# A hybrid decoder layer: own buffer for a sigmoid, 252-column products, an earlier weight load, banded diagonal sums and another PSUM bank

## The chip, the cores and the metric

The kernel runs on one core of a Trainium2 chip. The metric is the device time of one execution in microseconds (us), the median of several. Engines are named as the profile names them: PE is TensorE's matmul and PEld its weight load, DVE is VectorE, ACT is ScalarE, POOL is GpSimd, and SP issues the DMAs.

## The reference

One inference step of a hybrid layer for 1024 prompt tokens and 8 samples of 4 tokens each. 16 learned meta tokens stand ahead of the prompt and are dropped from its output; in all 1072 tokens of width 1024.

```python
# h = h + W_out( sum_b sigmoid(gate_b(x)) * W_b( silu(zgate_b(x)) * mixer_b(x) ) ),  x = RMSNorm(h)
# four branches, each 512 wide, fed from one combined input projection:
#   A: GLA      gated linear attention, 4 heads of dk 64, dv 128
#   B: HGRN2    4 heads of 128
#   C: mLSTM    4 heads of 128
#   D: convolution: GLU -> causal depthwise conv of width 31 -> LayerNorm -> swish -> pointwise
# gla_chunk: S_t = diag(exp g_t) S_{t-1} + k_t^T v_t ;  o_t = q_t S_t
```

It gives the outputs of both groups and the end states of all four branches.

## The kernel before

Numbers are kept near fp32 by splitting each operand into a high part in the rounded type fp32r and the rest as a low part. A product is then three matmuls: high by high, low by high, high by low. Weights are split by ACT (`wh`, L138) and POOL or DVE (`wl`, L139); `E=V` asks for DVE.

The stages follow one another in time. Up to about 100 us, `x` is normalised, transposed (`xt`, L174) and split (`xh` L178, `xl` L179) in three blocks of 384, 384 and 304 tokens; four gate projections (`gate_direct`) and small projections (`small`) run beside it. Then comes the pair stage until about 500 us: 19 calls of `pair`, each of which computes a 256 x 1072 projection with 7 products instead of 8, in the manner of Strassen. A product is 2 halves of 268 tokens, 4 blocks of k, 3 matmuls: 24, and 168 a pair. The products land in PSUM tiles `sa` to `sd`, and the callbacks `c11`, `c12`, `c22` and `c21` take the four quarters of the result. The names `p1`, `u2`, `u3` and `p5` are their sums, made on DVE.

Four of the 19 pairs (`conv_pair`) make the convolution's input `u`; the other 15 (`pair_to`) make gates and send them out by DMA. In `conv_pair`, `c11` puts a sigmoid of the first quarter into `u` (ACT, L349), `c12` multiplies `u` in place (DVE, L352), and `conv_taps` then runs 31 DVE operations over `u` (L388 for 30 of them), with a priority that lets them fill DVE's free time. `u` and the sum `y` have one buffer each, so that a convolution's `u` is free only when the last tap of the one before has read it.

From 500 us the mixers follow: four HGRN2 units, two GLA units (from about 850 us), four mLSTM units, and at last the branch and gate products until the end. In the GLA units `vtok` projects values (`vf`), transposes them by `to_tok` (`tta`, evacuated by ACT as `vt`, L539) and splits a small transposed piece (`v9p`, L557). `linear_unit` makes diagonal sums (`dg`, L760) with `prod` as weights and a matrix of 2 columns, in plain fp32, which is two instructions a matmul. `lv` (L636) and `lvt` (L640) are the small products of the attention levels.

No order is written out by hand. A scheduler simulates the program's timeline when it is built and sets each engine's order, so a change in one place moves rows elsewhere. PSUM tiles come from pools: `acc_tile` from one with 3 buffers, which the projections use too, `mmt` from another with 3.

Of the kernel before, what the change touches and what calls it, by code (L numbers as in the profile page):

```python
# [27 lines left out]
P = 128  # L28
# [37 lines left out]
def trunk(ctx, tc, hx, w_in, w_sm, w_br, w_out, pk, wgk2, mlb, fnorm, s_gla, s_hg, s_c, s_n, s_m, s_cv,  # L66
# [80 lines left out]
    xh = xp.tile([P, KD, NT], F32R, name="xh", tag="xh")  # L147
    xl = xp.tile([P, KD, NT], F32R, name="xl", tag="xl")
    with tc.tile_pool(name="x0", bufs=9, side="right", reuse_waits="tile") as x0:
        hs = []  # L150

        def load_h(i):
            n = min(P, NT - i * P)
            h = x0.tile([P, D], F32, name="h", tag="h")
            DMA.dma_start(h[:n], hx[i * P:i * P + n, :])
            hs.append((h, n))

        for i0 in (0, 3, 6):
            for i in range(i0, i0 + 3):
                load_h(i)  # L160
                h, n = hs[i]
                ss = x0.tile([P, 1], F32, name="ss", tag="ss", bufs=9)
                sq = x0.tile([P, D], F32, name="sq", tag="sq", bufs=1)
                S.activation(sq[:n], h[:n], AF.Square, accum_out=ss[:n])
                V.tensor_scalar(ss[:n], ss[:n], 1.0 / D, EPS, ALU.mult, ALU.add)
                rs = rsqrt(ss[:n])
                V.tensor_scalar(h[:n], h[:n], rs, None, ALU.mult)
            if i0 == 0:
                raw0 = load_raw(w_in, OFF["gate"])
            for k in range(KD):  # L170
                ps = mmt("xt")
                t = 0
                for h, n in hs[i0:i0 + 3]:
                    T.transpose(ps[:, t:t + n], h[:n, k * P:(k + 1) * P], ident[:n, :n])  # L174
                    t += n
                nw = col("norm_w", k)
                hi = xh[:, k, i0 * P:i0 * P + t]
                S.activation(hi, ps[:, :t], AF.Identity, scale=nw)  # L178
                V.scalar_tensor_tensor(xl[:, k, i0 * P:i0 * P + t], ps[:, :t], nw, hi, ALU.mult, ALU.subtract)  # L179
            if i0 == 0:  # L180
                w0 = split_w(raw0, E=V)

    def mm3(ps, wh, wl, ah, al, kd, order=None):
        for i, k in enumerate(order or range(kd)):
# [23 lines left out]
    def stt(tag, name=None):  # L208
        return gtl(tag, [P, HT], STB[tag], name)
# [39 lines left out]
        xs.update(a11=a(0, 0), a12=a(KH, 0), a22=a(KH, HT), s1=a(0, HT), s2=(sh[:, 0], sl[:, 0]),  # L249
                  s3=(sh[:, 1], sl[:, 1]), s4=(sh[:, 2], sl[:, 2]))  # L250

    def pair(c0, c1, c11, c12, c22, c21):


        wp = pools["gph"]
        r0, r1 = load_raw(w_in, c0), load_raw(w_in, c1)
        b11, b21, b12, b22 = r0[:, :KH], r0[:, KH:], r1[:, :KH], r1[:, KH:]
        w1 = split_w(r0)
        ta = wp.tile([P, KD, P], F32, name="ta", tag="tt", bufs=2)
        t1, t2 = ta[:, :KH], ta[:, KH:]  # L260
        V.tensor_tensor(t1, b12, b11, ALU.subtract)
        V.tensor_tensor(t2, b22, t1, ALU.subtract)
        w2 = split_w(ta, E=V, pool="gph")
        tb = wp.tile([P, KD, P], F32, name="tb", tag="tt", bufs=2)
        t3, t4 = tb[:, :KH], tb[:, KH:]
        V.tensor_tensor(t3, b22, b12, ALU.subtract)
        V.tensor_tensor(t4, b21, t2, ALU.subtract)
        w3 = split_w(tb, E=V, pool="gph")
        w4 = split_w(r1[:, KH:], KH)
        ps = lambda tag: [pools["ps"].tile([P, 512], F32, name="s" + tag, tag="a" if tag == "a" else "r",  # L270
                                           bufs=2 if tag == "a" else 5)[:, :HS] for _ in range(2)]

        def prod(w, o, x, s, out, start, stop):
            xa, xb = (t[:, :, s * HS:(s + 1) * HS] for t in xs[x])
            for k in range(KH):
                wh, wl = w[0][:, o + k], w[1][:, o + k]
                T.matmul(out, wh, xa[:, k], start=start and k == 0, stop=False, skip_group_check=True)  # L277
                T.matmul(out, wh, xb[:, k], start=False, stop=False, skip_group_check=True)  # L278
                T.matmul(out, wl, xa[:, k], start=False, stop=stop and k == KH - 1, skip_group_check=True)  # L279

        h = lambda t, s: t[:, s * HS:(s + 1) * HS]
        a, b, c = ps("a"), ps("b"), ps("c")
        p1, u2 = stt("p1"), stt("u2")
        for s in range(2):
            prod(w1, 0, "a11", s, a[s], True, True)
            S.activation(h(p1, s), a[s], AF.Copy)
        for s in range(2):
            prod(w2, KH, "s2", s, b[s], True, True)
            V.tensor_tensor(h(u2, s), h(p1, s), b[s], ALU.add)
        p5, u3 = stt("p5"), stt("u3")  # L290
        for s in range(2):
            prod(w2, 0, "s1", s, c[s], True, True)
            S.activation(h(p5, s), c[s], AF.Copy)
        for s in range(2):
            prod(w1, KH, "a12", s, a[s], False, True)
            c11(s, a[s])
        d = ps("d")
        for s in range(2):
            prod(w3, 0, "s3", s, d[s], True, True)
            S.activation(h(u3, s), d[s], AF.Copy)  # L300
        V.tensor_tensor(u3, u3, p5, ALU.add)
        V.tensor_tensor(u3, u3, u2, ALU.add)
        c22(u3)
        for s in range(2):
            prod(w4, 0, "s4", s, c[s], False, True)
            V.tensor_tensor(h(p1, s), h(u2, s), c[s], ALU.add)
        c12(p1)
        for s in range(2):
            prod(w3, KH, "a22", s, d[s], False, True)
            V.tensor_tensor(h(u2, s), h(u2, s), d[s], ALU.add)  # L310
        c21(u2)

    def pair_to(sec, i, dst, func, times=False, base=0):

        g11 = stt("g11")
        o = OFF[sec] + i * P
        i += base

        def c11(s, ps):
            g = g11[:, s * HS:(s + 1) * HS]  # L320
            S.activation(g, ps, func)
            if times:
                V.tensor_tensor(g, ps, g, ALU.mult)
            if s == 1:
                DMA.dma_start(dst[i, :, 0:HT - NM], g11[:, NM:])

        def rest(j, second):
            def ev(t):
                if times:
                    sg = stt("sg")  # L330
                    S.activation(sg, t, func)
                    V.tensor_tensor(t, t, sg, ALU.mult)
                elif func != AF.Copy:
                    S.activation(t, t, func)
                if second:
                    DMA.dma_start(dst[j, :, HT - NM:], t)
                else:
                    DMA.dma_start(dst[j, :, 0:HT - NM], t[:, NM:])
            return ev

        pair(o, o + P, c11, rest(i + 1, False), rest(i + 1, True), rest(i, True))

    def conv_pair(i):
        u = gtl("u", [P, UW + NSEQ * 34])
        us = u[:, UW:].rearrange("p (s x) -> p s x", x=34)
        G.memset(u[:, 0:30], 0.0)

        def c11(s, ps):
            S.activation(u[:, 30 + s * HS:30 + (s + 1) * HS], ps, AF.Sigmoid)  # L349

        def c12(t):
            V.tensor_tensor(u[:, 30:30 + HT], t, u[:, 30:30 + HT], ALU.mult)  # L352

        held = []

        def c21(t):
            S.activation(t, t, AF.Sigmoid)
            m = NP - HT
            V.tensor_tensor(u[:, 30 + HT:UW], held[0][:, :m], t[:, :m], ALU.mult)
            x3 = lambda v: v[:, m:].rearrange("p (s j) -> p s j", j=NDEC)  # L360
            V.tensor_tensor(us[:, :, 30:34], x3(held[0]), x3(t), ALU.mult)

        pair(OFF["cb"] + i * P, OFF["ca"] + i * P, c11, c12, held.append, c21)
        return u, us
# [73 lines left out]
                DMA.dma_start(fscr[p, :, t0:t0 + n], gx)  # L438

    open_pool("gph", bufs=1)  # L440
    gate_direct(0, w=w0)
    gate_direct(1)
    small()
    for j in range(2, NDIR):
        gate_direct(j)
# [129 lines left out]
    def vtok(sec, i, ones_col=False):  # L575
        vf = tl("vf", [P, 9 * P], 1)
        G.memset(vf[:, NT:NT + 16], 0.0)
        x9 = tl("x9", [P, 3, NT - NP], 1)

        def ev(ps, t0, n):  # L580
            S.activation(vf[:, t0:t0 + n], ps, AF.Copy)
            if t0 + n == NT:
                S.activation(x9, ps[:, NP - t0:].unsqueeze(1).broadcast_to([P, 3, NT - NP]), AF.Copy)

        proj(sec, i, GA, ev)
        vt = tl("vt", [P, 9, 129], 4)
        (to_tok_v(vf, vt) if ones_col else to_tok(vf, vt, True))
        v9 = split3(x9, 1, "v9", 4, acc_tile("v9p"))
        if ones_col:
            G.memset(vt[:, :, 128:129], 1.0)  # L590
        return vt, v9
# [162 lines left out]
    def linear_unit(uid, qv, nh, k, f, prod, vts, s0, epss, finish, pout, sout):  # L754
        rw = P // nh
        if nh == 2:
            ps = mmt("dg")
            for c in range(9):
                n = csz(c)
                T.matmul(ps[:n, 2 * c:2 * c + 2], prod[:, c * P:c * P + n], onesb, start=True, stop=True)  # L760
            dg = tl("dg", [P, 18], 2)
            V.tensor_copy(dg[:, 0:16], ps[:, 0:16])
            V.tensor_copy(dg[:TAIL, 16:18], ps[:TAIL, 16:18])
# [583 lines left out]
```

## Time and profile before

| | |
|---|---|
| median of 3 runs | 1597.33 us (1597.06 to 1597.72) |
| the profiled execution | 1597.18 us |
| its span in the profile | 1595.4 us |
| mean granted TensorE clock | 0.989 |
| PE, DVE, ACT, POOL busy | 98%, 65%, 35%, 30% of the span |

The profile is one execution. A row of a group gives busy us and the mean of one in ns, then the idle time before them and what ended it. A row of a timeline gives the start and duration in us, and in brackets the idle time ahead of it and its releaser. A matmul's duration is from issue to the last result; since matmuls overlap, their rate is read from how many start in a stretch.

### The profile page before, as it was taken

To read this page: it belongs to the slowest core of one execution; us is meant where nothing else is said; L and a number is where in the kernel's file an instruction comes from. 1 tells how busy PE (TensorE), PEld (TensorE's weight loads), DVE (VectorE), ACT (ScalarE), POOL (GpSimd) and SP (SyncE) were. 2 spreads that over 40 slices of the span, in tenths; PEclk is the share of its full clock that TensorE was granted. 3 is DMA by queue.
4 is the path that set the end of the run, shared out by engine and by line. 5 is a ranking of instruction groups with operands and counts; after the bars stand their busy time and mean duration, and the time that the engine had idled before them with its cause. 6 is when DMAs were issued, how large, how long until landed. Compare 5 with 4: busy or idle time off the path is not lost.

```text
span 1595.4 us, 30033 instructions
## 1 busy us (share of the span) xinstructions
PE 1558.2 (98%) x12366; PEld 1496.5 (94%) x12366; DVE 1035.6 (65%) x1827; ACT 554.0 (35%) x1095; POOL 470.9 (30%) x418
## 2 busy tenths in 40 slices
PE   7999999899999999999999999999999999999998
PEld 6999999899999899999998998999999999999886
DVE  7959979999996446444544565476665646744533
ACT  6534343243433333323424323323323244422211
POOL 2222322123223232223232323222322313877300
PEclk9999999999999999999999999999999999999999
DMA  5423233231337113131323132144323277676231
GB/s 190 133 80 101 92 91 107 88 108 51 110 100 236 42 48 104 56 100 56 104 60 94 55 97 82 49 148 135 117 72 88 89 248 224 179 236 208 80 111 54
DMA packets 190572, 176.40 MB, mean 111 GB/s; under 512 B 9260, under 2 KB 164800, under 8 KB 190436
## 3 DMA queue, kind: packets, MB, share of 16 engines
q1 hardware_dynamic: 190436, 174.49, 35.6%
q8 instruction: 97, 1.59, 0.4%
q14 instruction: 39, 0.32, 0.1%
HBM read 122.45 MB, written 52.00 MB: 109 GB/s over the span
## 4 chain that ended last, share of the span: by engine, by line
PE 78%; DVE 16%; issue 3%; DMA 2%; ACT 1%; SPq 0%; DVEq 0%; POOLq 0%; ACTq 0%
PE acc L187 18%; PE acc L185 18%; PE acc L186 18%; DVE y L388 7%; PE lv L636 2%; DVE wl L139 2%; PE sa L277 1%; PE sa L278 1%; PE sa L279 1%; PE sc L278 1%; PE sc L277 1%; PE sc L279 1%; PE sd L279 1%; PE op L800 1%; PE sd L278 1%
## 5 line engine op out<-in xcount | busy, mean ns | idle before, releaser
L139 POOL TENSOR_TENSOR wl<-wraw,wh 128x1024 fp32r<-128x1024 f32 (+1 forms) x124 | 272.2, 2196 | 632.7 <-ACT wh L138 628.0
L185 PE MATMUL acc<-xh,wh 128*128 128x352 f32 (+2 forms) x1320 | 437.5, 332 | 2.1 <-ACT vt L539 1.2
L187 PE MATMUL acc<-xh,wl 128*128 128x352 f32 (+2 forms) x1320 | 436.7, 331 | 0.0
L186 PE MATMUL acc<-xl,wh 128*128 128x352 f32 (+2 forms) x1320 | 435.5, 330 | 0.0
L185 PEld LDWEIGHTS acc<-xh,wh 128*128 128x128 f32 x1320 | 251.7, 191 | 5.6 <-ACT vt L539 1.9
L187 PEld LDWEIGHTS acc<-xh,wl 128*128 128x128 f32 x1320 | 251.0, 190 | 3.2 <-issue 0.9
L186 PEld LDWEIGHTS acc<-xl,wh 128*128 128x128 f32 x1320 | 251.4, 190 | 1.8 <-issue 0.7
L388 DVE SCALAR_TENSOR_TENSOR y<-u,pkt,y 128x1024 f32<-128x1024 f32 x120 | 191.2, 1593 | 0.7
L138 ACT ACTIVATE wh<-wraw 128x512 fp32r<-128x512 f32 (+1 forms) x125 | 110.4, 883 | 231.0 <-PE acc L186 135.8
L185 PE MATMUL acc<-zh,wh 128*128 128x352 f32 x384 | 124.5, 324 | 0.0
L186 PE MATMUL acc<-zl,wh 128*128 128x352 f32 x384 | 124.3, 324 | 0.0
L187 PE MATMUL acc<-zh,wl 128*128 128x352 f32 x384 | 124.2, 324 | 0.0
L277 PE MATMUL sa<-xh,wh 128*128 128x268 f32 x304 | 88.7, 292 | 6.6 <-ACT u L349 6.3
L278 PE MATMUL sa<-xl,wh 128*128 128x268 f32 x304 | 88.2, 290 | 0.0
L279 PE MATMUL sa<-xh,wl 128*128 128x268 f32 x304 | 87.8, 290 | 0.0
L651 DVE TENSOR_TENSOR q<-q,tot 128x256 f32<-128x256 f32 (+3 forms) x96 | 46.4, 483 | 54.5 <-PE lv L636 53.7
L1179 POOL TENSOR_TENSOR mix<-mix,gt 128x352 f32<-128x352 f32 x72 | 73.1, 1030 | 28.9 <-DVE gt L1178 25.7
L185 PEld LDWEIGHTS acc<-zh,wh 128*128 128x128 f32 x384 | 72.2, 188 | 0.4 <-DVE gt L1178 0.4
L187 PEld LDWEIGHTS acc<-zh,wl 128*128 128x128 f32 x384 | 72.3, 188 | 0.0
L186 PEld LDWEIGHTS acc<-zl,wh 128*128 128x128 f32 x384 | 72.2, 188 | 0.0
L277 PEld LDWEIGHTS sa<-xh,wh 128*128 128x128 f32 x304 | 58.3, 192 | 7.3 <-ACT u L349 6.8
L1178 DVE TENSOR_TENSOR gt<-acc,gt 128x352 f32<-128x352 f32 x72 | 36.2, 518 | 39.5 <-PE acc L187 36.6
(393 smaller groups left out, 3367.3 us busy)
## 6 DMA issues: line engine op xcount, KB each, us to landing
wraw<-w_in SPq DMA_DIRECT2D x92, 512.0 KB, 3.9
gt<-gscr SPq DMA_DIRECT2D x30, 528.0 KB, 4.7
gscr<-gd SPq DMA_DIRECT2D x60, 176.0 KB, 1.8
zr<-zscr SPq DMA_DIRECT2D x16, 528.0 KB
wraw<-w_br SPq DMA_DIRECT2D x32, 256.0 KB, 2.9
gt<-sscr SPq DMA_DIRECT2D x12, 528.0 KB, 4.1
zscr<-gt SPq DMA_DIRECT2D x12, 528.0 KB, 2.6
sscr<-u SPq DMA_DIRECT2D x16, 268.0 KB, 2.3
```

Source lines behind the costliest of these rows:

```text
L138: S.activation(hi[:, :kd], raw[:, :kd], AF.Copy)
L139: (E or G).tensor_tensor(lo[:, :kd], raw[:, :kd], hi[:, :kd], ALU.subtract)
L185: T.matmul(ps, wh(k), ah(k), start=(i == 0), stop=False)
L186: T.matmul(ps, wh(k), al(k), start=False, stop=False)
L187: T.matmul(ps, wl(k), ah(k), start=False, stop=(i == kd - 1))
L277: T.matmul(out, wh, xa[:, k], start=start and k == 0, stop=False, skip_group_check=True)
L278: T.matmul(out, wh, xb[:, k], start=False, stop=False, skip_group_check=True)
L279: T.matmul(out, wl, xa[:, k], start=False, stop=stop and k == KH - 1, skip_group_check=True)
L388: V.scalar_tensor_tensor(ymain, u[:, NM + j:NM + j + NPR], w(j), ymain, ALU.mult, ALU.add)
L651: V.tensor_tensor(qx[:, :, 1], qx[:, :, 1], pv[r, :, 0:1].broadcast_to([rw, nb, h]), ALU.mult)
L1178: V.tensor_tensor(gt[:, t0:t0 + n], ps[:, :n], gt[:, t0:t0 + n], ALU.mult)
L1179: G.tensor_tensor(mixed[j][:, t0:t0 + n], mixed[j][:, t0:t0 + n], gt[:, t0:t0 + n], ALU.add)
```

## The change

1. `conv_pair` writes the sigmoid into a tile of its own, `g11` (a tag with 2 buffers that `pair_to` uses already), and `c12` multiplies by it into `u`.
2. `pair` takes `m`, which `pair_to` sets to the 16 meta tokens. In two of the seven products (`a12`, `s4`) the first half then leaves out its first 16 columns: 252 instead of 268.
3. The raw weights of gates 0 and 1 are both loaded with the first block of `x`; gate 0 is split behind k = 1 and gate 1 behind k = 5, both with DVE for the low part. Before, gate 1 was loaded and split by `gate_direct`.
4. The diagonal sums go in bands of 32 rows: 34 matmuls a GLA unit instead of 9.
5. `v9p` takes its PSUM tile from `mmt`.

```diff
@@ x preparation
-        hs = []
+        hs, wg01 = [], []
 ...
             if i0 == 0:
-                raw0 = load_raw(w_in, OFF["gate"])
+                raws = [load_raw(w_in, OFF["gate"] + j * P) for j in range(2)]
             for k in range(KD):
 ...
-            if i0 == 0:
-                w0 = split_w(raw0, E=V)
+                if i0 == 0 and k in (1, 5):
+                    wg01.append(split_w(raws[k // 4], E=V))
 ...
-    gate_direct(0, w=w0)
-    gate_direct(1)
+    for j in range(2):
+        gate_direct(j, w=wg01[j])
@@ pair
-        def prod(w, o, x, s, out, start, stop):
-            xa, xb = (t[:, :, s * HS:(s + 1) * HS] for t in xs[x])
+        def prod(w, o, x, s, out, start, stop, m=0):
+            m = m if s == 0 else 0
+            out = out[:, m:]
+            xa, xb = (t[:, :, s * HS + m:(s + 1) * HS] for t in xs[x])
 ...
-            prod(w1, KH, "a12", s, a[s], False, True)
+            prod(w1, KH, "a12", s, a[s], False, True, m)
 ...
-            prod(w4, 0, "s4", s, c[s], False, True)
+            prod(w4, 0, "s4", s, c[s], False, True, m)
@@ conv_pair
+        g11 = stt("g11")
 ...
-            S.activation(u[:, 30 + s * HS:30 + (s + 1) * HS], ps, AF.Sigmoid)
+            S.activation(g11[:, s * HS:(s + 1) * HS], ps, AF.Sigmoid)
 ...
-            V.tensor_tensor(u[:, 30:30 + HT], t, u[:, 30:30 + HT], ALU.mult)
+            V.tensor_tensor(u[:, 30:30 + HT], t, g11, ALU.mult)
@@ vtok
-        v9 = split3(x9, 1, "v9", 4, acc_tile("v9p"))
+        v9 = split3(x9, 1, "v9", 4, mmt("v9p"))
@@ linear_unit
-                T.matmul(ps[:n, 2 * c:2 * c + 2], prod[:, c * P:c * P + n], onesb, start=True, stop=True)
+                for b in range(0, n, 32):
+                    e = min(b + 32, n)
+                    T.matmul(ps[b:e, 2 * c:2 * c + 2], prod[:, c * P + b:c * P + e], onesb, start=True, stop=True,
+                             skip_group_check=True)
```

Line numbers behind the change: L277 to L279 become L280 to L282, L349 becomes L353, L352 L356, L388 L392, L539 L543, L557 L561, L581 L585, L636 L640, L640 L644, L760 L766, L902 L909, L903 L910, L842 L849.

The scheduler moves rows. First DVE at the third conv pair. Before, the last three taps of the second convolution, and `c12` (L352) behind them:

```order
L267 TENSOR_TENSOR tb<-wraw,ta 128x512
L139 TENSOR_TENSOR wl<-ta,wh 128x1024
L388 SCALAR_TENSOR_TENSOR y<-u,pkt,y 128x1024 x2
L359 TENSOR_TENSOR u<-u_2958,u_2904 128x504
L361 TENSOR_TENSOR u<-u_2958,u_2904 128x8x4
L352 TENSOR_TENSOR u<-p_2903,u 128x536
```

and now:

```order
L392 SCALAR_TENSOR_TENSOR y<-u,pkt,y 128x1024
L139 TENSOR_TENSOR wl<-ta,wh 128x1024
L392 SCALAR_TENSOR_TENSOR y<-u,pkt,y 128x1024
L356 TENSOR_TENSOR u<-p_2906,g_2872 128x536
L363 TENSOR_TENSOR u<-u_2961,u_2907 128x504
L365 TENSOR_TENSOR u<-u_2961,u_2907 128x8x4
```

The taps still stand ahead of `c12`, which reads `g11` (here `g_2872`) instead of `u`. Counted over the stage, 5 taps of the last convolution now stand behind the last pair's `u3` sum (L304; before L301), against 1.

Second, ACT in the first GLA unit, where the second head's values are evacuated (`vf`, `x`, `vt`). Before:

```order
L581 ACTIVATE vf<-acc 128x358
L902 ACT_TABLE_LOAD
L902 ACTIVATE ab<-ab 128x1072
L903 ACT_TABLE_LOAD
L903 ACTIVATE ab<-ab 128x1072
L581 ACTIVATE vf<-acc 128x358
L842 ACT_TABLE_LOAD
L842 ACTIVATE f<-f 128x1072
L138 ACTIVATE wh<-wraw 128x1024
L581 ACTIVATE vf<-acc 128x356
```

and now:

```order
L585 ACTIVATE vf<-acc 128x358 x2
L138 ACTIVATE wh<-wraw 128x1024
L585 ACTIVATE vf<-acc 128x356
L587 ACTIVATE x_9418<-acc 128x96
L543 ACTIVATE vt<-tta 128x4x128 x2
L543 ACTIVATE vt<-tta 48x128
L564 ACTIVATE v_9521<-v9p 96x128
L217 ACTIVATE gd<-acc 128x352
L909 ACT_TABLE_LOAD
L909 ACTIVATE ab<-ab 128x1072
```

The chain of the forget gate (L902, L903, L842 with three table loads) has moved behind the evacuations and a gate's `gd`.

Third, SP at the start. Before, gate 1's weights were issued behind all loads of `h`:

```order
L155 DMA h<-hx 128x1024 x3
L132 DMA wraw<-w_in 128x8x128
L155 DMA h<-hx 128x1024 x5
L155 DMA h<-hx 48x1024
L132 DMA wraw<-w_in 128x8x128
```

and now they are ahead of six of them:

```order
L155 DMA h<-hx 128x1024 x3
L132 DMA wraw<-w_in 128x8x128 x2
L155 DMA h<-hx 128x1024 x5
L155 DMA h<-hx 48x1024
```

On PE the rows of the first gates keep their places.

More of the change, by code (lines that the diff above doesn't have):

```diff
@@ L250, in combine_x, with pair @@
                   s3=(sh[:, 1], sl[:, 1]), s4=(sh[:, 2], sl[:, 2]))
-    def pair(c0, c1, c11, c12, c22, c21):
+    def pair(c0, c1, c11, c12, c22, c21, m=0):
         wp = pools["gph"]
@@ L339, in rest @@
             return ev
-        pair(o, o + P, c11, rest(i + 1, False), rest(i + 1, True), rest(i, True))
+        pair(o, o + P, c11, rest(i + 1, False), rest(i + 1, True), rest(i, True), NM)
     def conv_pair(i):
         u = gtl("u", [P, UW + NSEQ * 34])
+        g11 = stt("g11")
         us = u[:, UW:].rearrange("p (s x) -> p s x", x=34)
```

## The prediction

> **What bounds the kernel now.** I read the page first: busy shares and the chain that ended last.
>
> ```profile
> span 1595.4 us, 30033 instructions
> PE 1558.2 (98%) x12366; PEld 1496.5 (94%) x12366; DVE 1035.6 (65%) x1827; ACT 554.0 (35%) x1095; POOL 470.9 (30%) x418
> ...
> PE 78%; DVE 16%; issue 3%; DMA 2%; ACT 1%; SPq 0%; DVEq 0%; POOLq 0%; ACTq 0%
> ...
> L388 DVE SCALAR_TENSOR_TENSOR y<-u,pkt,y 128x1024 f32<-128x1024 f32 x120 | 191.2, 1593 | 0.7
> ```
>
> PE is busy 98% of the span, and yet DVE holds 16% of the chain, most of it with the convolution taps of L388. So there are two ways to gain: shorter PE work, or fewer of PE's waits. PE's waits over the whole program come next (us in total, times, longest).
>
> ```profile
> PE xt L174 <- DVE ss L165: 8.1, 2, 7.9
> PE sa L277 <- ACT u L349: 6.3, 2, 4.8
> PE lv L636 <- DVE k L652: 4.8, 3, 1.9
> PE tta L538 <- ACT vf L581: 2.3, 1, 2.3
> PE xt L174 <- DVE xl L179: 2.2, 1, 2.2
> PE acc L185 <- ACT vt L539: 1.2, 4, 0.3
> ...
> PE sd L279 <- DVE wl L139: 0.9, 2, 0.5
> PE sc L277 <- DVE p L306: 0.8, 2, 0.4
> ```
>
> The second row is a wait for the sigmoid that the change moves, the fourth lies where a GLA unit's rows are reordered, the sixth is the bank of the `v9p` transpose. Then stretches of the pair stage (busy us and count for PE, PEld, DVE, ACT, POOL, then PE's granted clock).
>
> ```profile
> 175.00:200.00 25.00, 23.48 (x189) 23.27 (x188) 24.80 (x31) 9.17 (x17) 6.03 (x3) 1.00 0.30 97
> 275.00:300.00 25.00, 19.18 (x143) 18.18 (x142) 24.79 (x25) 6.37 (x11) 5.86 (x5) 0.94 0.19 54
> 300.00:325.00 25.00, 25.00 (x191) 24.98 (x190) 21.16 (x31) 8.57 (x18) 2.90 (x3) 0.92 0.36 112
> 400.00:425.00 25.00, 25.00 (x204) 24.98 (x204) 25.00 (x32) 11.81 (x24) 6.24 (x2) 1.00 0.43 132
> 220.00:490.00 270.00, 263.01 (x2093) 261.23 (x2092) 264.38 (x311) 95.08 (x181) 64.76 (x28) 0.99 0.32 97
> ```
>
> Undisturbed, 204 matmuls of 268 columns fit into 25 us, one per 122.5 ns. The stretches from 175, 275 and 300 fall short of that by 15, 61 and 13. The last row warns: DVE is busy 264.38 of 270 us there, so PE is little ahead of a second bound.
>
> **1. The sigmoid's own buffer.** The big wait, on three engines:
>
> ```profile
> 298.52 0.68 ACT L349 ACTIVATE u<-sa 128x268 f32<-128x268 f32 x2 [5.02 <-DVE y L388]
> ...
> 293.80 4.68 DVE L388 SCALAR_TENSOR_TENSOR y<-u,pkt,y 128x1024 f32<-128x1024 f32 x2
> ...
> 298.97 0.59 PE L277 MATMUL sa<-xh,wh 128*128 128x268 f32 x1 [4.83 <-ACT u L349]
> ```
>
> ACT may not write `u` before the last tap of the convolution before has read it; PE stands for the PSUM bank that ACT should have emptied. With `g11` that order is gone for ACT. What goes: 6.3 us of waits, and the half clock behind them. That is 13 x 0.1225 = 1.6 us in the stretch from 300; 0.5 in the last microsecond before 300 (PE runs 1.03 us there after its wait, at half rate); and 0.3 at 175 (15 x 0.1225 = 1.8, less the second wait, 6.3 - 4.8 = 1.5). Together 8.7 us.
>
> What is late next is `c12`, the DVE product that still writes `u` and still stands behind the taps. PE needs its DVE results only some 36 matmuls (4.4 us) after a conv pair, so a delay under that is covered. But DVE has 5.6 us free in the 270. The new order helps: behind the last pair's `u3` sum there now stand 5 taps instead of 1, so 4 x 1.59 = 6.4 us of taps leave the stage. DVE then has 258.0 us of work for a stretch that PE wants to do in 270 - 8.7 - 2.6 (part 2) = 258.7. That leaves no slack, and the waits of 0.9 and 0.8 us on `wl` and `p` show how such lateness looks. I set 2.0 us for their growth (between 0 and 9, the latter being a rival). Net **-6.7**.
>
> **2. 252 columns.** 15 pairs x 2 products x 4 k x 3 = 360 matmuls lose 16 columns. Rows by width (mean ns of one behind the bar):
>
> ```profile
> L277 PE MATMUL sb<-sh,wh 128*128 128x268 f32 x152 | 43.7, 287 | 0.1
> L185 PE MATMUL acc<-xh,wh 128*128 128x358 f32 x368 | 121.8, 331 | 0.0
> L185 PE MATMUL acc<-woh,mh 128*128 128x512 f32 x128 | 50.7, 396 | 0.0
> ...
> L1066 PE MATMUL sdn<-nmask,k 96*128 96x8 f32 x4 | 0.7, 171 | 0.0
> L640 PE MATMUL lvt<-q,k 128*16 128x8 f32 x16 | 1.6, 174 | 0.0
> ```
>
> (396 - 287)/(512 - 268) = 0.45 ns a column, or 7.2 ns for 16. 360 x 7.2 gives **-2.6**. It is 0 if DVE paces the stage, and at most -6.7 by the closest spacing seen for weights 128 wide (104 ns, part 3): 360 x (122.5 - 104). No fp32r row lies between 8 and 268 columns, so the price of 252 is an extension of the slope; the nearest row, 268, is 16 columns away.
>
> A page gives that bound otherwise. The Trainium skill, "TensorE: Matmul & The Clock Gate", section "LDWEIGHTS (loading the stationary operand)", puts a weight load at columns/1.2 ns, so 107 ns for 128 columns (an estimate by that page), and the term could not pass -5.6; the 104 ns of the trace is near it.
>
> **3. Diagonal sums in bands.** Nine products of 128 rows (18 instructions in plain fp32) become 34 of 32 or 16 rows (68).
>
> ```profile
> 853.91 2.02 PE L760 MATMUL dg<-onesb,prod 128*128 128x2 f32 x18
> ...
> 857.33 0.86 PE L636 MATMUL lv<-q,k 128*32 128x32 f32 x46
> ...
> 853.00:861.00 8.00, 8.00 (x109) 7.26 (x108) 3.32 (x7) 3.04 (x7) 4.84 (x4) 0.79 0.26 68
> 963.00:970.00 7.00, 6.90 (x43) 6.14 (x42) 3.69 (x10) 3.93 (x8) 6.12 (x5) 0.76 0.50 139
> ```
>
> The old ones start (2.02 - 0.25)/17 = 104 ns apart. `lv` has weights of 32 columns as the bands will: (0.86 - 0.20)/45 = 15 ns apart. So 68 x 15 = 1.0 us instead of 1.9, and I take 0.8 saved in each of the two GLA units, -1.6 (0 if bands cost 28 ns each). Both bursts are followed by half clock: 0.79 over 8 us and 0.76 over 7 are each 1.7 us lost at most. A shorter burst removes part of it; I take 1.0 for both. **-2.6**, between 0 and -5.0.
>
> A rule speaks against this. The Trainium skill, the same page, section "Part 3: Packing small matmuls — row/col tiling", says that a weight load overlaps matmuls in flight only where the row group differs, and bands share all rows. With its 27 ns for 32 columns (an estimate) the loads alone would take 1.8 us, nothing would be saved, and the sum would end 1.6 us higher. The 15 ns of `lv`, which shares all rows too, says otherwise, and I go by the row.
>
> **4. Another bank for `v9p`.** The four waits `acc <- vt` total 1.2 us. In the other pool a transpose waits for other readers; I take **-1.0** (0 to -1.2).
>
> **5. GLA reorder.** In unit 0, ACT's chain of L902, L903 and L842 with its table loads stood between two `vf` evacuations and now stands behind them.
>
> ```profile
> 875.36 0.66 PE L538 MATMUL tta<-ident,vf 128*128 128x128 f32 x4 [2.30 <-ACT vf L581]
> ...
> 871.00:881.00 10.00, 7.70 (x127) 6.67 (x126) 9.44 (x15) 7.10 (x12) 6.08 (x10) 0.83 0.21 55
> ...
> 975.98 0.26 DVE L998 SCALAR_TENSOR_TENSOR dmt<-r1b,cols,negt 48x48 f32<-48x48 f32 x1 [3.25 <-DMA r1b<-rscr]
> ```
>
> The 2.30 us go, and of the clock loss (0.83 over 10 us, at most 1.7) I take 1.2. The chain is now a possible delay for `gd` evacuations, where PE has about 9 us of other rows. In unit 1, DVE's wait for `r1b` ahead of the `q` products stays: `dmt` keeps its place in the new order. Since everything after 500 us is reordered a little, I put 1.7 against it. **-1.8** (+4 to -4).
>
> **6. The start.** Gate 1's raw weights are loaded ahead of six `h` loads, and their low part moves from POOL to DVE.
>
> ```profile
> 9.50 1.06 ACT L138 ACTIVATE wh<-wraw 128x1024 fp32r<-128x1024 f32 x1 [0.57 <-DMA wraw<-w_in]
> 10.73 1.22 DVE L139 TENSOR_TENSOR wl<-wraw,wh 128x1024 fp32r<-128x1024 f32 x1
> 20.94 2.36 POOL L139 TENSOR_TENSOR wl<-wraw,wh 128x1024 fp32r<-128x1024 f32 x1 [1.43 <-ACT wh L138]
> 20.96 2.62 DVE L420 TENSOR_TENSOR wg<-wgr,wg 16x256 fp32r<-16x256 f32 x1
> 25.06 0.90 PE L174 MATMUL xt<-ident,h 128*128 128x128 f32 x3 [2.23 <-DVE xl L179]
> ```
>
> Costs: 1.06 us on ACT and 1.22 on DVE ahead of the first `xl`, and the later `h` rows are squared that much later. Gains: ACT's 1.10 us at 19.8 goes, and L420, which took 2.62 us beside POOL's 2.36, has no POOL beside it, so the second block's `xl` needn't wait for it. ACT's table load also moves behind. Gate 1's matmuls keep their place among gate 0's, so sooner weights alone bring nothing. **0** (-3 to +3).
>
> **Sum.** -6.7 - 2.6 - 2.6 - 1.0 - 1.8 + 0 = -14.7. The profiled execution took 1597.18 us (span 1595.4 and 1.8 around it), 0.15 under the median of 1597.33, so they are taken as one: **1582.5 us**.
>
> **Rivals.**
> (a) *Slower: 252 columns leave the fast pace.* All fp32r rows of weight have 268 columns or more. If the narrower ones ran like plain fp32, the price is in this row:
>
> ```profile
> 822.11 1.96 PE L814 MATMUL op<-s,qblk 128*48 128x128 f32 x16
> ```
>
> (1.96 - 0.27)/15 = 112 ns for 128 columns, two instructions each: 441 ns for 252 instead of 122.5, 360 x 318 = +115, so 1585.1 + 115 = 1700 us. It decides from (1597.2 - 1585.1)/360 = 34 ns extra on. Against it: `sdn`, fp32r with 8 columns, takes 171 ns in one instruction beside 174 for each of plain fp32's two. But that row is too short to tell paces apart. 9%.
> (b) *DVE paces the pair stage.* PE's waits move from `u` to `p`, `u2` and `wl`, and parts 1 and 2 give together only 2.5 us: 1597.2 - 2.5 - 2.6 - 1.0 - 1.8 = 1589. For it stand DVE's 98%, against it the taps moved out and the stretches where PE loses nothing beside a full DVE (400 to 425). 20%.
> (c) *Everything goes.* 8.7 + 2.6 + 3.3 + 1.2 + 4.0 = 19.8: 1577. 9%.
> (d) *The reorder eats it.* New stalls at the start (+3) and in the GLA units (+4 instead of -1.8) on top of (b): about 1598. 7%.
>
> **Chances.** My forecast has 55%, with 1579 to 1587 as its own range. The range of 1576 to 1593 holds it, (b) and most of (c); (a), (d) and the far end of (c) lie outside, under 20%. A change under 0.2% (1594.1 to 1600.5) can't be told from none. Faster: 55 + 20 + 9 = 84%; same 7%; slower 9%.
>
> **What would show it.** Part 1: no PE wait for ACT's sigmoid, 204 matmuls in each 25 us from 275 to 325, clock 1.00. If (b), rows `PE sa, sb, sc or sd <- DVE` of several us. Part 2: 252-column rows near 280 ns with the same count; if (a), a PE stage 115 us longer with no waits. Part 3: dg x68 in 1.0 us and a higher clock behind it. Part 5: no `tta <- vf` wait. Part 6: the `xt <- xl` wait and PE's first gate as before. I am wrong if DVE turns PE's new speed into waits, or if the unmeasured width has another price.

## The result and the profile after

The changed kernel took 1585.47 us (median of 4, 1583.30 to 1588.61) beside 1597.53 for the kernel before on the same chip: a ratio of 0.9919, with an interval of 0.9891 to 0.9946. Forecast were 1582.5 in a range of 1576 to 1593. On another chip the same two gave 0.9937 (0.9925 to 0.9949). Its profiled execution took 1584.46, and that is what the traces below explain: 12.7 us less than the 1597.18 of before.

The head of its page, with the engines' shares of the chain:

```profile
span 1582.6 us, 30248 instructions
PE 1545.5 (98%) x12466; PEld 1483.6 (94%) x12466; DVE 1037.5 (66%) x1828; ACT 554.3 (35%) x1096; POOL 471.4 (30%) x417
...
PE 77%; DVE 15%; issue 3%; DMA 2%; ACT 1%; POOL 0%; DVEq 0%; SPq 0%; POOLq 0%; ACTq 0%
```

PE is 98% busy as before; all engines do the same work in a shorter span. PE's waits over the program:

```profile
PE xt L174 <- DVE ss L165: 9.1, 3, 8.5
PE lv L640 <- DVE k L656: 7.3, 6, 2.1
PE acc L185 <- ACT xh L178: 2.3, 2, 1.7
PE xt L174 <- DVE xl L179: 1.6, 2, 0.9
PE sb L280 <- DVE p L309: 1.5, 2, 0.9
PE sd L280 <- DVE u L292: 1.3, 2, 0.7
PE tta L542 <- ACT vf L585: 1.0, 2, 0.8
PE sa L280 <- DVE g L326: 1.0, 2, 0.5
```

The sigmoid's 6.3 us and the four waits for `vt` are gone. In their place stand small waits of the pair products for DVE's `p`, `u` and `g`, and `lv`'s wait for `k` grew from 4.8 to 7.3 us. The pair stage in stretches (busy us and count for PE, PEld, DVE, ACT, POOL; granted clock):

```profile
275.00:300.00 25.00, 25.00 (x206) 25.00 (x205) 24.86 (x26) 7.85 (x15) 7.44 (x5) 1.00 0.23 67
300.00:325.00 25.00, 25.00 (x206) 24.98 (x206) 22.97 (x31) 6.28 (x13) 6.95 (x4) 1.00 0.48 137
350.00:375.00 25.00, 23.17 (x183) 22.52 (x182) 24.28 (x27) 7.94 (x16) 6.23 (x2) 1.00 0.31 85
400.00:425.00 25.00, 23.83 (x192) 23.61 (x193) 25.00 (x34) 10.24 (x21) 6.25 (x2) 1.00 0.30 92
325.00:475.00 150.00, 144.65 (x1156) 142.32 (x1155) 148.78 (x178) 53.86 (x108) 39.86 (x16) 1.00 0.30 91
```

Where the old kernel started 143 and 191 matmuls, there are 206 now, at full clock. But from 325 on it starts fewer in most stretches than it could, and fewer than the old kernel's 204 in 400 to 425, while DVE is busy 148.78 of 150 us.

To place the difference I take the times of the same PE rows in both traces: the first matmul of the first pair, the last of the pair stage, the first `lv` of the fourth HGRN unit, the first `yt` behind the mLSTM units, and the end of the span. Each number is the time against the same row of before, in us. The kernels of the experiments are in the same table. Executions of one kernel differ by several us (the kernel before took 1592.38 to 1601.19 in 23 of them on one chip), and each row is one execution: differences of about a microsecond between rows say little.

| profiled execution of | first pair | pair stage ends | 4th HGRN unit | behind mLSTM | end |
|---|---|---|---|---|---|
| the changed kernel | +2.0 | -5.8 | -10.8 | -12.6 | -12.8 |
| the same again (e12) | +1.5 | -6.3 | -11.3 | -11.8 | -11.5 |
| e1 sigmoid only | -1.5 | -8.1 | -8.2 | -13.3 | -12.6 |
| e2 columns only | -0.7 | -2.3 | -4.0 | -4.4 | -4.0 |
| e3 start only | +0.5 | -0.3 | -0.3 | -1.0 | -1.1 |
| e4 all but the start | -0.7 | -7.2 | -11.8 | -12.7 | -12.8 |
| e5 bands only | -1.4 | -1.9 | -1.9 | -4.1 | -3.6 |
| e6 bank only | -1.8 | -1.7 | -6.6 | -9.9 | -9.6 |
| e7 half the taps | +1.7 | -14.5 | -19.5 | -21.7 | -20.9 |
| e8 128 columns | +1.6 | -6.1 | -10.7 | -12.6 | -12.3 |
| e9 w3 on POOL | +0.1 | +13.4 | +8.4 | +12.1 | +12.1 |
| e10 small r1 | +0.7 | -7.0 | -11.9 | -11.3 | -10.5 |
| e11 three mended | -1.6 | +12.9 | +8.0 | +8.0 | +9.7 |

So the changed kernel loses 2.0 us at the start, gains 7.8 in the pair stage, 5.0 in the first three HGRN units, 1.8 from there through the mLSTM units, and 0.2 behind them: -12.8 of span.

### The profile page after: what moved, and what is told of

It is laid out like the page before. It is cut to its first block, busy times and chain, and to the rows that moved or that the text cites. A ratio compares the mean times of both kernels' runs of the same rounds, so it can differ in the third digit from the quotient of the medians.

```text
span 1582.6 us, 30248 instructions
## 1 busy us (share of the span) xinstructions
PE 1545.5 (98%) x12466; PEld 1483.6 (94%) x12466; DVE 1037.5 (66%) x1828; ACT 554.3 (35%) x1096; POOL 471.4 (30%) x417
## 4 chain that ended last, share of the span: by engine, by line
PE 77%; DVE 15%; issue 3%; DMA 2%; ACT 1%; POOL 0%; DVEq 0%; SPq 0%; POOLq 0%; ACTq 0%
PE acc L185 17%; PE acc L186 17%; PE acc L187 17%; DVE y L392 4%; PE lv L640 2%; PE sa L280 2%; PE sa L281 2%; PE sa L282 2%; PE sc L280 1%; PE sc L281 1%; PE sc L282 1%; PE sd L281 1%; PE sd L280 1%; PE sd L282 1%; DVE so L576 1%
## 5 line engine op out<-in xcount | busy, mean ns | idle before, releaser
L139 POOL TENSOR_TENSOR wl<-wraw,wh 128x512 fp32r<-128x512 f32 (+1 forms) x123 | 277.2, 2256 | 634.8 <-ACT wh L138 599.3
L392 DVE SCALAR_TENSOR_TENSOR y<-u,pkt,y 128x1024 f32<-128x1024 f32 x120 | 192.8, 1607 | 0.6
L280 PE MATMUL sa<-xh,wh 128*128 128x268 f32 (+1 forms) x304 | 87.4, 288 | 1.7 <-DVE g L326 1.0
L282 PE MATMUL sa<-xh,wl 128*128 128x268 f32 (+1 forms) x304 | 86.6, 285 | 0.0
L281 PE MATMUL sa<-xl,wh 128*128 128x268 f32 (+1 forms) x304 | 86.6, 285 | 0.0
L280 PEld LDWEIGHTS sa<-xh,wh 128*128 128x128 f32 x304 | 57.3, 188 | 2.3 <-DVE g L326 1.4
```

The lines of the kernel that those rows point to most:

```text
L139: (E or G).tensor_tensor(lo[:, :kd], raw[:, :kd], hi[:, :kd], ALU.subtract)
L392: V.scalar_tensor_tensor(ymain, u[:, NM + j:NM + j + NPR], w(j), ymain, ALU.mult, ALU.add)
```

## The experiments

Every experiment is built by the same scheduler, so each has an order of its own; that turned out to matter. Ratios are to the kernel before on the same chip.

**e1, the sigmoid's buffer alone.** Edit of the kernel before:

```diff
+        g11 = stt("g11")
-            S.activation(u[:, 30 + s * HS:30 + (s + 1) * HS], ps, AF.Sigmoid)
+            S.activation(g11[:, s * HS:(s + 1) * HS], ps, AF.Sigmoid)
-            V.tensor_tensor(u[:, 30:30 + HT], t, u[:, 30:30 + HT], ALU.mult)
+            V.tensor_tensor(u[:, 30:30 + HT], t, g11, ALU.mult)
```

> The kernel before with part 1 alone (the sigmoid's own buffer). My theory: PE's waits for the sigmoid (6.3 us) and the half clock behind them (2.4 us) go, and DVE, which is nearly full in the pair stage, gives some of it back as waits of PE for p and u. In the profile 5 to 8 us less before the end of the pair stage, total 1589 to 1592. Rival A: what the whole change gained came mostly from elsewhere and DVE gives all of this back: total 1596 to 1599. Rival B: this part alone is worth the whole change: 1584 to 1586.

Ratio 0.9949 (0.9930 to 0.9969), profiled execution 1584.80, the fastest of six (median 1588.17). By the ratio the part gives 8 us, 1589, and the theory holds. In the profile it gains 6.6 us from the first pair to the end of the stage, as my theory has it. Another 5.0 us lie between the fourth HGRN unit and the end of mLSTM, where this edit touches nothing: the order moved there.

**e2, the 252 columns alone.**

```diff
-        def prod(w, o, x, s, out, start, stop):
-            xa, xb = (t[:, :, s * HS:(s + 1) * HS] for t in xs[x])
+        def prod(w, o, x, s, out, start, stop, m=0):
+            m = m if s == 0 else 0
+            out = out[:, m:]
+            xa, xb = (t[:, :, s * HS + m:(s + 1) * HS] for t in xs[x])
```

> The kernel before with part 2 alone (252 columns in 360 of the pair stage's matmuls). My theory: 278 ns against 286 in their rows, so 7 to 8 ns each, 2.6 us in the pair stage as long as PE sets its pace; the sigmoid's wait of 4.8 us stays. Total 1594 to 1596. Rival: since the sigmoid's wait is for DVE's taps, PE only arrives sooner and waits longer; then nothing is left: 1597 to 1598.

Ratio 0.9972 (0.9960 to 0.9984), profiled 1593.20. The stage is 1.6 us shorter, between theory (2.6) and rival (nothing): a wait for the sigmoid grew from 6.3 to 7.1 us. Another 1.6 us came in the HGRN units, again by order.

**e3, the early load alone, and e4, all but the early load.**

```diff
-                raw0 = load_raw(w_in, OFF["gate"])
+                raws = [load_raw(w_in, OFF["gate"] + j * P) for j in range(2)]
```

> The kernel before with part 3 alone (both gates' weights loaded with the first block of x). My theory: the first pair starts 2 us later than before, as in the whole change, and nothing gives it back: total 1598 to 1600. Rival: the late start in the profile of the whole change was chance of that execution (its first h landed 0.6 us later): the first pair starts within 0.7 us of before, total 1597 to 1598.

> The whole change without part 3. My theory: the start is as before the change, so it gains 2 us on the whole change: 1582 to 1584 where that takes 1584.5 to 1585.5. Rival: the pair stage is paced by DVE from its middle on and swallows the earlier start: 1584 to 1586.

e3: ratio 1.0002 (0.9987 to 1.0017), profiled 1596.09, first pair 0.5 us later than before: nearer to the rival. But one profile is a poor measure here. In the table, seven executions without the early load (before, e1, e2, e4, e5, e6, e11) start their first pair between -1.8 and 0.0 us, -1.1 on the mean; the seven with it (the changed kernel, e3, e7 to e10, e12) between +0.1 and +2.0, +1.2 on the mean. The two groups don't overlap, if barely: the early load costs some 2.3 us at the start, with a spread of about 1 us to either side from one execution to the next. PE's row that waits for the second block's `xh` parts the two groups more clearly: it starts at 22.3 to 22.8 us in the seven without the load and at 24.9 to 25.5 in the seven with it. At the end of the program e3's ratio shows no cost.

e4: ratio 0.9935 (0.9918 to 0.9953), profiled 1584.39. Its 2.7 us of lead at the first pair are 1.3 at the end of the stage and 0.1 behind mLSTM. Rival right: the waits of DVE's pace and of the GLA units take them back.

**e5, the bands alone.**

```diff
-                T.matmul(ps[:n, 2 * c:2 * c + 2], prod[:, c * P:c * P + n], onesb, start=True, stop=True)
+                for b in range(0, n, 32):
+                    e = min(b + 32, n)
+                    T.matmul(ps[b:e, 2 * c:2 * c + 2], prod[:, c * P + b:c * P + e], onesb, ...)
```

> The kernel before with part 3 of the sum alone (the diagonal sums in bands of 32 rows). My theory: the burst dg takes 0.7 us instead of 2.0 as in the whole change, so 1.2 to 1.3 us go in each of the two GLA units, and the clock behind it stays higher; 2.5 to 4 us less from the first GLA unit to the end, nothing ahead of it: 1593 to 1595. Rival: the products of the levels that follow wait for DVE, not for dg; then PE only waits longer there and the profile shows the same end: 1596.5 to 1597.5.

Ratio 0.9980 (0.9967 to 0.9992), profiled execution 3.6 us of span shorter, of which 1.4 were there at the first pair and so by chance. From the fourth HGRN unit through mLSTM it gains 2.2 us, a little under the 2.5 to 4 expected. The clock behind the bursts did more than expected. The prediction's two stretches of the kernel before were granted 0.79 and 0.76; the same stretches at e5's two bursts (the second is mixed with other products there):

```profile
851.20:859.20 8.00, 7.99 (x172) 7.11 (x171) 5.05 (x9) 3.06 (x7) 4.95 (x4) 1.00 0.26 70
961.00:968.00 7.00, 6.90 (x106) 5.94 (x104) 4.65 (x10) 2.65 (x7) 6.09 (x4) 1.00 0.51 140
```

In all traces the same holds: the five kernels without bands (before, e1, e2, e3, e6) are granted 0.76 to 0.84 over such 8 or 7 us at each burst, the nine with bands 1.00 at both. PE was busy all through the first of the old stretches, so no wait within it brought the lower clock, and with the burst in bands it is gone. That makes more to win than the 2.2 us gained. Part of it went into waits: in the stretch from 770 to 1300 us `tta` waits 3.9 us for `vf` instead of 2.3, and `lv` 3.8 for `k` instead of 2.9, as the rival has it.

**e6, the other bank alone.**

```diff
-        v9 = split3(x9, 1, "v9", 4, acc_tile("v9p"))
+        v9 = split3(x9, 1, "v9", 4, mmt("v9p"))
```

> The kernel before with the other bank for v9p alone. My theory: the four waits of the projections for the transposed values' evacuation (1.2 us) go, 0.3 us in each HGRN unit: 1596 to 1596.5. The 1.9 us wait of lv in the first HGRN unit and its half clock, which are gone in the whole change, stay. Rival: that wait goes too, since this part moves rows there: about 5 us less, 1592 to 1593.

Ratio 0.9939 (0.9922 to 0.9956): this one word, expected to give 1 us, gives nearly 10 (in the profiled execution 1.8 of its 9.6 us were there at the first pair and so by chance). The rival was right and even it was short. Before, in the first HGRN unit, on DVE and PE:

```profile
546.12 1.26 DVE L904 SCALAR_TENSOR_TENSOR lf<-lf,ct 4x1072 f32<-4x1072 f32 x1 [1.27 <-ACT ct L903]
...
548.54 0.44 PE L636 MATMUL lv<-q,k 128*32 128x16 f32 x32 [1.90 <-DVE k L652]
...
540.00:560.00 20.00, 18.10 (x343) 16.95 (x342) 12.30 (x32) 7.10 (x8) 3.82 (x4) 0.91 0.18 55
```

and in e6, on DVE (a row of the timeline) and in the same stretch:

```profile
543.31 1.26 DVE L904 SCALAR_TENSOR_TENSOR lf<-lf,ct 4x1072 f32<-4x1072 f32 x1 [0.80 <-ACT ct L903]
...
540.00:560.00 20.00, 19.97 (x391) 18.55 (x390) 13.81 (x36) 9.42 (x15) 4.08 (x4) 1.00 0.27 83
```

`lf` is a row of mLSTM's forget gate that waits for ACT and has nothing to do with HGRN. Before, it stood between two levels of `q` and `k` products on DVE, and PE's `lv` stood behind it, 1.90 us and then half clock (0.91 over 20 us). With the other bank the scheduler put it ahead of the level products, where the wait costs PE nothing. Of the 4.9 us gained in the HGRN units, 3 x 0.3 are the bank's own waits. The rest, 3.9, is nearly what this wait and its clock cost: 1.90 us and 9% of 20 us. In the changed kernel `lf` (L911 there) stands ahead of the level products too, and every kernel with the new bank gains 4.6 to 5.0 us in these units, while e1, e3 and e5 gain 0.1 at most and e2 1.6.

**e7, half the taps.** The taps run on 512 of the 1024 prompt columns; the other half of the convolution's sum is left out.

```diff
-            V.scalar_tensor_tensor(ymain, u[:, NM + j:NM + j + NPR], w(j), ymain, ALU.mult, ALU.add)
+            V.scalar_tensor_tensor(ymain[:, :512], u[:, NM + j:NM + j + 512], w(j), ymain[:, :512], ALU.mult, ALU.add)
```

> The whole change, with the taps of L392 on 512 of 1024 columns: the other half of the convolution's sum is left out, and with it some 90 us of DVE's work in the pair stage. My theory: DVE's load is what gives the gain of the pair stage back (PE waits for p, u and g, about 5 us between 325 and 475 us): without it PE starts 204 to 207 matmuls in every 25 us of the stage and the stage ends 4 to 6 us sooner against its start (398 us from the first pair to the last instead of 402.5). Rival: PE's waits there come from the order of rows or from the weights' DMAs and stay: 401 to 403 us.

The same 150 us as above, and one of the stretches:

```profile
350.00:375.00 25.00, 25.00 (x205) 25.00 (x204) 17.99 (x28) 9.99 (x18) 4.26 (x4) 1.00 0.21 65
...
325.00:475.00 150.00, 150.00 (x1225) 149.99 (x1224) 125.95 (x184) 58.59 (x108) 28.84 (x16) 1.00 0.35 106
```

1225 matmuls instead of 1156, PE without a gap, and 394.1 us from the first pair to the end of the stage where the changed kernel takes 402.5 and the old one 410.3. So DVE's taps hold back 8.4 us, more than I expected, and the rival is out. (This is one execution, and a halved tap also stands half as long ahead of a sum, so DVE's load and the place of the taps aren't told apart.) The 69 missing matmuls are 69 x 0.122 = 8.4 us too, though PE's idle time in the stretch is only 5.35. A matmul's row lasts some 285 ns while they start 122 ns apart, so by my reading a wait that shows as idle time has already cost some 160 ns more, and one shorter than that doesn't show at all.

**e8, 128 columns.** 124 more columns of two products are left out of the gates' first half.

```diff
-        pair(o, o + P, c11, rest(i + 1, False), rest(i + 1, True), rest(i, True), NM)
+        pair(o, o + P, c11, rest(i + 1, False), rest(i + 1, True), rest(i, True), 140)
```

> The whole change, with 128 columns instead of 252 in the same 360 matmuls: 124 more columns of two products are left out, so that the first half of the gates is not complete. My theory by the slope of 0.45 ns a column with the floor of 104 ns that matmuls with 128 columns of weights show: 104 to 110 ns from start to start where 252 columns take 115, 2 to 4 us less of PE work, some of it lost to waits for DVE. Rival, the slow one of my prediction a little further down: fp32r matmuls below some width run at the pace of plain fp32, 112 ns twice, and the stage gets 35 to 45 us longer.

The stretch from 95 to 170 us, where PE doesn't wait, in the kernel before, the changed one and e8:

```profile
95.00:170.00 75.00, 75.00 (x609) 74.98 (x608) 64.14 (x79) 28.11 (x53) 17.13 (x8) 1.00 0.27 79
95.00:170.00 75.00, 75.00 (x613) 74.98 (x612) 63.41 (x79) 28.49 (x54) 15.84 (x8) 1.00 0.30 86
95.00:170.00 75.00, 75.00 (x616) 74.98 (x615) 62.61 (x78) 28.14 (x54) 15.95 (x8) 1.00 0.29 83
```

By the first matmuls of pairs 2 and 5, three pairs of `pair_to` take 62.73, 62.13 and 61.81 us. With 72 narrower matmuls in them that is 8.3 ns less each for 252 columns and 12.8 for 128, against 124.5 on the mean of 268: about 116 and 112 ns from start to start. So no fall to the pace of plain fp32. The slope of 0.45 ns a column ends on the way: 124 columns fewer save only 4.5 ns. The whole stage is no shorter than with 252 columns (402.6 us against 402.5, one execution each): behind DVE's pace, shorter PE work was worth nothing here.

**e9, w3 on POOL.**

```diff
-        w3 = split_w(tb, E=V, pool="gph")
+        w3 = split_w(tb, pool="gph")
```

> The whole change, with the low part of one of the pair's four weight tiles (w3) made on POOL instead of DVE: 1.22 us of 21 less for DVE in every pair. My theory: with the taps halved the stage took 394 us from the first pair to its end instead of 402.5, so DVE's load holds back 8.4 us; with 23 us of it on POOL, 4 to 8 us of that come back: 1577 to 1581 where the whole change takes 1584.5 to 1585.5. Rival: POOL, which takes 2.2 us for such a tile, is late with w3, or slows DVE beside it; PE then waits for wl on POOL, and nothing or less than 2 us is gained.

Ratio 1.0071 (1.0057 to 1.0085): slower than before. Groups of the pair stage, first of the changed kernel (DVE), then of e9 (DVE, POOL, and two of PE's waits):

```profile
L392 DVE SCALAR_TENSOR_TENSOR y<-u,pkt,y 128x1024 f32<-128x1024 f32 x89 | 143.8, 1615 | 0.4
L139 DVE TENSOR_TENSOR wl<-ta,wh 128x1024 fp32r<-128x1024 f32 x12 | 14.6, 1214 | 0.1
L304 DVE TENSOR_TENSOR u<-u,p 128x536 f32<-128x536 f32 x12 | 9.6, 797 | 0.0
```

```profile
L392 DVE SCALAR_TENSOR_TENSOR y<-u,pkt,y 128x1024 f32<-128x1024 f32 x85 | 146.5, 1723 | 0.6
L139 DVE TENSOR_TENSOR wl<-ta,wh 128x1024 fp32r<-128x1024 f32 x11 | 17.8, 1617 | 0.0
L304 DVE TENSOR_TENSOR u<-u,p 128x536 f32<-128x536 f32 x11 | 13.7, 1241 | 0.0
...
L139 POOL TENSOR_TENSOR wl<-tb,wh 128x1024 fp32r<-128x1024 f32 x12 | 38.6, 3214 | 49.8 <-ACT wh L138 49.8
...
PE sb L280 <- DVE p L309: 11.0, 5, 4.0
PE sd L280 <- DVE u L292: 7.9, 6, 2.2
```

The tile takes POOL 3.2 us, not 2.2, and DVE's rows grow: a tap by 108 ns, a `wl` by 0.4 us, a `u` sum by 0.44. PE's waits for DVE's `p` and `u` went up from 2.8 to 18.9 us, and none of its waits is for POOL. So the second half of the rival holds, and far beyond the "nothing" that it gave: POOL's work slows DVE's.

The means hide how. In the changed kernel too, single rows of DVE and the POOL rows beside them read:

```profile
404.86 3.08 DVE L392 SCALAR_TENSOR_TENSOR y<-u,pkt,y 128x1024 f32<-128x1024 f32 x1
410.73 1.27 DVE L392 SCALAR_TENSOR_TENSOR y<-u,pkt,y 128x1024 f32<-128x1024 f32 x1
...
402.84 6.25 POOL L139 TENSOR_TENSOR wl<-wraw,wh 128x1024 fp32r<-128x1024 f32 x2 [8.66 <-ACT wh L138]
```

From 220 to 485 us, 58 of the 89 taps have no POOL instruction beside them and take 1.27 to 1.29 us; the 19 that have one beside them for at least half their time take 2.8 on the mean and 3.4 at most. In e9 the lone taps take 1.27 to 1.29 us as well, but 29 of 85 stand beside POOL. The Trainium skill, "SBUF — State Buffer", section "SBUF: two separate sides", says that a DVE instruction with two SBUF inputs and a POOL instruction that reads SBUF take a shared pair of ports as an exclusive lock, for the whole instruction. The trace agrees: a tap beside POOL takes up to 2.2 us longer. So does the start of the program before, where L420 took 2.62 us beside a POOL instruction of 2.36; the same row takes 0.42 in the changed kernel (L424), without POOL.

**e10, a small tile for the early use of r1b.**

```diff
+        r1t = tl("r1t", [TAIL, TAIL], 1)
+        DMA.dma_start(r1t, rscr[h:h + 1, NPR:NT].broadcast_to([TAIL, TAIL]))
-        V.scalar_tensor_tensor(dmt, r1b[:TAIL, NPR:NT], cols[:TAIL, 8, h:h + 1], negt, ALU.add, ALU.min)
+        V.scalar_tensor_tensor(dmt, r1t, cols[:TAIL, 8, h:h + 1], negt, ALU.add, ALU.min)
```

> The whole change, with a tile of 48x48 of its own for the one early use of r1b (dmt, L1005), so that DVE no longer waits 5.1 us for the large load in the second GLA unit with the products of the levels behind it. My theory: lv's waits for k in that unit (2.1, 1.2 and 0.8 us) and the half clock behind them go, 4 to 6 us less before the mLSTM units, total 1579 to 1581. Rival: the products wait for the q and k ahead in any case and the stall only moves into the mLSTM unit: 1584 to 1586.

Ratio 0.9918 (0.9904 to 0.9933), not to be told apart from the changed kernel's 0.9937 (0.9925 to 0.9949) of e12 on that chip. PE's waits from 840 to 1300 us:

```profile
PE lv L640 <- DVE k L656: 4.9, 5, 1.5
PE spt L1018 <- DVE v L565: 2.3, 1, 2.3
PE dc L1034 <- DVE dmt L1019: 1.0, 1, 1.0
```

The last `lv` of the GLA units comes 5.2 us sooner than in the changed kernel (14.6 against 9.4 before the same row of before), but `spt <- v`, 0.3 us there, is 2.3 now, and behind mLSTM nothing of the lead is left. The rival was right.

**e11, three things at once** (no early load, w3 on POOL, the small tile), and **e12, the changed kernel again.**

> The whole change without part 3 of its list (the early load at the start), with w3 on POOL and the small tile for dmt. My theory: with neither DVE in the pair stage nor the load of r1b in the GLA unit to take it back, the 2.4 us of the start stay gained too: 1572 to 1577. Rival: as with the start alone, the gains are swallowed by other waits further down: 1580 to 1585.

> The changed kernel once more, unaltered, on the chip of the three above. Theory: 1583 to 1587, and a first pair that starts within 1 us of 91.9 us. Rival for the start: its 2 us were chance of one execution, and the first pair starts at 88 to 90 us like those without the early load.

e11: ratio 1.0052 (1.0039 to 1.0065), since it holds e9's mistake; the theory is out. Beside e9 it is 1.7 us ahead at the first pair, 0.5 at the end of the pair stage, 4.1 behind mLSTM and 2.4 at the end, in one execution each: whether the gains of the other two parts survive isn't shown. e12: 1586.32, as expected, and a first pair at 91.5 us: the theory on the start, not its rival. None of the kernels that compute the whole layer is clearly faster than the changed one.

## Why the prediction was right, and where its steps were not

The forecast of -14.7 us stands against -12.7 in the profiled execution; the range held. Step by step, the total is better than its parts: the HGRN units gave 4.0 us more than forecast, while the pair stage fell short by 1.5, the GLA units by 2.6 and the start by 2.0. That the sum came within 2 us is in part luck.

1. *The sigmoid and the columns* (parts 1 and 2: -6.7 and -2.6, together -9.3): -7.8. The mechanism was right: the wait is gone, the clock is 1.00 from 275 to 325 us, and the narrower matmuls cost 8.3 ns less each where I had 7.2. Two terms were mis-sized. What there was to win was 16.2 us (e7), not 8.7 + 2.6 = 11.3; e7 also lacks the small waits that I left standing. And DVE took back 8.4 instead of the 2.0 that I set. I wrote that DVE's 258.0 us of work in a stretch of 258.7 leaves no slack, and still set 2.0. Neither figure holds, besides. The 258.7 takes off the second wait (1.5 us, and 0.3 behind it), which lies ahead of 220 us. And the 258.0 rests on a wrong count: the 5 taps instead of 1 stand behind the `u3` sum of the 18th of the 19 pairs. Behind that of the last pair there is none in either trace; the last tap starts at 481.8 us before and at 486.7 now, the last `u3` sum at 495.0 and 489.3. So no tap left the stage, and DVE is as full as before:

```profile
220.00:485.00 265.00, 259.65 (x2094) 257.29 (x2093) 261.33 (x306) 91.97 (x182) 66.65 (x28) 1.00 0.32 95
```

   Part of rival (b) came true. I also overlooked what made the sigmoid's big wait so long. Of the two taps in front of it (4.68 us from 293.80 in my list), the first alone took 3.36 us and the second 1.29. POOL in the kernel before, at the same time:

```profile
293.57 2.51 POOL L139 TENSOR_TENSOR wl<-wraw,wh 128x1024 fp32r<-128x1024 f32 x1 [14.06 <-ACT wh L138]
```

   By the taps of e9's section, some 2.1 of the 4.83 us are DVE held up by POOL. And of DVE's 16% of the chain the taps of L388 hold 7%, less than half.
2. *fp32r below 268 columns* (rival a): out, down to 128 columns (e8). The load time of 107 ns for 128 columns (an estimate by the Trainium skill, "TensorE: Matmul & The Clock Gate", section "LDWEIGHTS (loading the stationary operand)") lies 5 ns under the 112 found there.
3. *The bands* (part 3: -2.6). The burst itself did what was expected, in the changed kernel and beside the old row:

```profile
858.55 0.73 PE L766 MATMUL dg<-onesb,prod 128*32 128x2 f32 x68
```

   (0.73 - 0.17)/67 = 8.4 ns apart, below even the 15 ns of `lv`. The rule that spoke against it (the Trainium skill, the same page, "Part 3: Packing small matmuls — row/col tiling": loads overlap matmuls in flight only where the row group differs) does not agree with this row; at 27 ns a load (an estimate by that page) the burst would have taken 1.8 us. Whether the rule or the load time is off, the row doesn't show. The half clock behind the burst, of which I took 1.0 us for both units, goes whole (1.00 instead of 0.79 and 0.76). Alone (e5) the bands give 2.2 us from the fourth HGRN unit through mLSTM, while PE's waits there grew by 2.5.
4. *The bank* (part 4: -1.0). The step that failed by most: alone it gives 9.6 us, and in the whole change the first three HGRN units gain 5.0. Its own waits were priced right (0.3 us a unit); what I didn't see is that `lv`'s wait of 1.9 us, the third row of my list of waits, was made by a stray row of another unit on DVE and would go when the order there changed. It is not that any change does it: with the orders of e1, e3 and e5 nothing is gained there.
5. *GLA* (parts 3 and 5: -4.4 together): -1.8, and -0.5 in e12. The 2.30 us of `tta` are 0.84 now. The term that failed is the 1.7 us set against the reorder: from 770 to 1300 us `lv` waits 7.3 us for `k` instead of 2.9. One row in front of these products is DVE's wait for `r1b`, which I said would stay; in the changed kernel:

```profile
966.23 0.26 DVE L1005 SCALAR_TENSOR_TENSOR dmt<-r1b,cols,negt 48x48 f32<-48x48 f32 x1 [5.13 <-DMA r1b<-rscr]
```

   5.13 us against 3.25. With the same order there it is 4.1 to 5.0 in e4, e7, e8, e9 and e12; in e2, e3 and e5 it is 3.0 to 4.1, in e1 1.1 and in e6 1.9. e1 and e6 gain more in these units than the whole change, but that this row is the reason isn't shown: e10 takes the wait away and keeps nothing of its lead.
6. *The start* (part 6: 0): +2.0 in this execution, some 2.3 on the mean. The step that failed is setting the gains even with the cost: the cost fell on ACT ahead of the second block's `xh`, the gain on DVE. Now, on DVE, ACT and PE:

```profile
12.95 1.23 DVE L139 TENSOR_TENSOR wl<-wraw,wh 128x1024 fp32r<-128x1024 f32 x1 [0.38 <-ACT wh L138]
...
24.87 2.46 ACT L178 ACTIVATE xh<-xt,pkt 128x384 fp32r<-128x384 f32 x5
...
25.50 0.66 PE L185 MATMUL acc<-xh,wh 128*128 128x352 f32 x1 [1.68 <-ACT xh L178]
27.06 0.90 PE L174 MATMUL xt<-ident,h 128*128 128x128 f32 x3 [0.90 <-DVE xl L179]
```

   The second block's `xh` starts at 24.87 instead of 21.76: the last squares of `h` come 1.3 us later, and the table load and a `gd`, 1.28 and 0.46 us, stand ahead of it now. I had the table load moving behind. PE's wait for this `xh` is 1.68 us. The gain that I set against it is there (L424 takes 0.42 us instead of 2.62), but it freed DVE where ACT was late. 0.6 us of this execution's +2.0 come from the first `h`, whose squares start at 5.70 us instead of 5.08.

The parts alone gain 12.6, 4.0, 1.1, 3.6 and 9.6 us in their profiles, 30.9 together, and the whole change 12.8. By the ratios of all executions they give about 8, 4.5, 0, 3 and 10 us, some 25, and the whole change 13 on one chip and 10 on the other. They aren't additive. By the table, 5.0 of the 30.9 us were there at the first pair, by chance. In the pair stage the parts give 9.3 us and the whole 7.8, in the HGRN units 6.7 and 5.0. From there through mLSTM they give 11.7 and the whole 1.8: there each part got an order of its own by the scheduler, and what in the order of the whole change costs these units most wasn't tested apart from e10.

## What to carry to other kernels

When a second engine is 98% busy in a stage, a gain of the first is worth only what the second has free: look for less work for it (e7) before shortening the first's (e8). Moving its work to a third engine can cost more than it frees (e9): compare single rows of the second engine with and without the third beside them before counting its free time. Under a scheduler that sets the order anew, look in the list of waits for those that a stray row makes, and expect a one-word edit to move them; a part's price alone is then no measure of the part. And try a part on its own before it goes in with four others: the early load makes the first pair 2 us later, which the total didn't show, and alone it gains nothing (e3).

## What the runs showed of the hardware

- A POOL instruction holds up DVE's instructions beside it: a tap of 1.27 us took up to 3.4 beside a weight split on POOL (changed kernel, 19 of 89 taps with a mean of 2.8). With 3.2 us more of POOL per pair, the taps' mean rose from 1615 to 1723 ns and that of the `u` sums from 797 to 1241 (e9).
- A burst of matmuls with 2 columns, 104 ns apart, was followed by a granted clock of 0.76 to 0.84 over 7 or 8 us in five kernels, with PE busy all through one of the stretches; the same sums in bands, 8.4 ns apart, by 1.00 in nine.
- fp32r matmuls with 128 columns of weights start about 124.5, 116 and 112 ns apart with 268, 252 and 128 columns; bands with 32 columns of weights start 8.4 ns apart.
- One and the same program need not get the same clock. From 840 to 880 us the changed kernel was granted 1.00, and again (e12), with 0.1 us less idle time, 0.96:

```profile
840.00:880.00 40.00, 35.81 (x526) 33.74 (x525) 21.00 (x42) 17.77 (x27) 15.07 (x26) 1.00 0.18 51
840.00:880.00 40.00, 35.94 (x517) 33.87 (x516) 20.16 (x40) 18.39 (x27) 15.67 (x26) 0.96 0.18 51
```
